# Normalising the recurrence's input behind its input product instead of ahead of it

## The chip, the cores and the metric

One core of one Trainium2 chip runs the whole program. The metric is the device time of one execution in microseconds (us), as the median of several runs.

## The reference

A trunk of two layers on 512 tokens of width 1024. Each layer adds half a SwiGLU feed-forward block, a token mixer, and half a feed-forward block again; layer 0 mixes with a gated recurrence, layer 1 with a spatial gating unit. The change lies where layer 0 passes from its first feed-forward block to the recurrence:

```python
def rms_norm(x, g):
    xf = x.astype(jnp.float32)
    y = xf * lax.rsqrt(jnp.mean(xf * xf, axis=-1, keepdims=True) + NORM_EPS)
    return (y * g.astype(jnp.float32)).astype(x.dtype)
...
def recurrent_mixer(x, w_in, conv_w, conv_b, gate_a_w, gate_a_b, gate_x_w, gate_x_b, lam, w_out):
    y, r = jnp.split(x @ w_in, 2, axis=-1)
    y = jax.nn.gelu(y)
    r = causal_depthwise_conv(r, conv_w, conv_b)
    h = rg_lru(r, gate_a_w, gate_a_b, gate_x_w, gate_x_b, lam)
    return (y * h) @ w_out
...
    h = h + 0.5 * swiglu(rms_norm(h, ffn1_norm[i]), ffn1_w_in[i], ffn1_w_out[i])
    hn = rms_norm(h, mix_norm[i])
```

The factor rsqrt(mean of squares) is one number per token; the gain g is one number per channel.

## The kernel before

Everything is float32, and each product is three matmuls: operands are split into a rounded high part and a rest, and high x high, high x low and low x high are summed. A split is one copy on ScalarE (`hi`, `whi`, `zh`; ACT in the profile) and one subtraction on VectorE (`lo`, `wlo`, `zl`; DVE). Most large products run as seven block products on 2 x 2 blocks, P1, P2, P5, P6, P3, P7 and Q4, which form sums in banks A, B, C and Q of PSUM. PSUM has six banks for these and for `r` and `gate`, and two more (`aux`) for transposes.

The kernel is written as a list of steps (`subs`). Each step has a weight tile, which is loaded and split three steps ahead, and matmuls. `hook(n, phase, fn)` puts other work at step n, in one of the phases pre, mid, rest (ahead of the step's matmuls), end and late (behind them). The order written there is the order in each engine's queue; each queue is worked off strictly in order. So work that waits on VectorE or ScalarE holds up everything behind it on that engine, the weight splits among it.

The feed-forward block's output product updates x in quarters of 256 tokens by 512 channels: A11 (tokens 0 to 255, channels 0 to 511), A12, A22, A21, in the order in which they are finished. Tokens lie on partitions in x, so the recurrence needs x transposed. In the kernel before, `TileNorm` does this a half at a time: when both quarters of a half are done, squares, a root and Newton steps give the factor `rt` of 256 tokens, four passes (two on ScalarE, two on VectorE) write normalised rows `xn`, 16 transposes put them into four banks `xt` (two of them `aux`), and eight pairs `zh`, `zl` read the banks out, with the gain, into the operand of the recurrence. `KORDER` is the order of the eight channel blocks k in that read-out and in the products.

The recurrence then has 8 blocks of 128 channels for `r` (blocks 0 to 3 first on the first half of the tokens, then on the second; 4 to 7 in one go) and 8 for `y`. An `r` block leaves its bank by one ScalarE pass (`rc`, the convolution's last tap) and three VectorE passes on the same bank (the other taps); `v` is then split, two gate products follow one or two steps later, and their sigmoids. A `y` block is copied out of its bank by VectorE (`drain`, blocks 0 to 2) and goes through gelu on ScalarE, or gelu reads the bank itself (blocks 3 to 7). `yh` multiplies it with the scanned state `h`, giving the left operand `a` of the output product, split as the first step of that product needs it.

## Time and profile before

| what | value |
|---|---|
| median of 3 runs | 1651.8 us (1651.05 to 1652.23) |
| span of the profiled execution | 1651.2 us |
| mean granted TensorE clock | 0.997 |
| TensorE matmul busy | 1621.7 us, 98% |
| VectorE busy | 1369.8 us, 83% |
| ScalarE busy | 1035.8 us, 63% |
| first `xn`, last `zl` | 345.3 us, 370.0 us |
| first `rc`, last `y` out of a bank | 375.7 us, 460.7 us |

The span is counted from the first to the last instruction of one execution; the runs' times also hold what lies around it, here 0.6 us. In rows of the time line the first number is the start in us, the second the duration (of the first to the last where several are put together, as "x8"); the bracket tells how long the engine had been idle and what ended that. Names are out<-in, with buffer numbers left out. A line number is often that of a small helper, so that the names tell more.

### The profile page before, as it was taken

What the parts mean: (1) busy time and instruction counts of PE and PEld (TensorE: products, weight loads), DVE (VectorE), ACT (ScalarE), POOL (GpSimd) and SP (SyncE); (2) the same over time, 40 slices, a digit from 0 to 9 for tenths busy, and PEclk for the clock granted to TensorE, in tenths of its full rate; (3) what the DMA queues carried; (4) which work ended last, traced back from release to release, by engine and by line L of the source; (5) the groups of instructions that cost most, each with busy time, mean ns of one, the idle gap of its engine ahead of it and who ended that gap; (6) DMA issues with size and microseconds to landing.
All of it is one profiled execution on the core that took longest, in us unless ns stands there. A gap on an engine that the chain in (4) does not pass through costs nothing. (4 is left out here: it accounts for less than half of the span.)

```text
span 1651.2 us, 20805 instructions
## 1 busy us (share of the span) xinstructions
PE 1621.7 (98%) x7475; PEld 1333.0 (81%) x7475; DVE 1369.8 (83%) x1814; ACT 1035.8 (63%) x1490; POOL 212.3 (13%) x193
## 2 busy tenths in 40 slices
PE   8999999989999999999999999999999999999997
PEld 6788888878878888888888888888888888888885
DVE  5898897787798897878988978878966988879777
ACT  6656656666957656556676565566864765665655
POOL 1111111200010111111101111111100011121120
PEclk9999999999999999999999999999999999999999
DMA  6767876952463876876838778768863557686693
GB/s 205 159 171 176 209 163 153 219 141 77 102 153 92 189 169 162 218 177 157 202 95 181 176 162 209 184 163 204 216 169 90 151 122 186 166 208 169 157 230 79
DMA packets 161288, 273.02 MB, mean 165 GB/s; under 512 B 11312, under 2 KB 37536, under 8 KB 161184
## 3 DMA queue, kind: packets, MB, share of 16 engines
q1 hardware_dynamic: 113856, 182.74, 35.9%
q0 software_dynamic: 45536, 87.10, 31.4%
q10 hardware_dynamic: 1792, 1.84, 0.4%
q8 instruction: 59, 0.97, 0.2%
q14 instruction: 45, 0.37, 0.1%
HBM read 269.55 MB, written 2.10 MB: 165 GB/s over the span
## 5 line engine op out<-in xcount | busy, mean ns | idle before, releaser
L96 ACT ACTIVATE whi<-raw 128x1024 fp32r<-128x1024 f32 (+1 forms) x539 | 556.4, 1034 | 423.0 <-PE A L347 108.2
L87 DVE TENSOR_TENSOR wlo<-raw,whi 128x1024 fp32r<-128x1024 f32 (+1 forms) x539 | 641.0, 1192 | 203.7 <-ACT whi L96 202.8
L346 PE MATMUL A<-whi,hi 128*128 128x512 f32 x984 | 393.1, 399 | 4.3 <-DVE x L93 4.3
L347 PE MATMUL A<-whi,lo 128*128 128x512 f32 x984 | 386.2, 392 | 3.6 <-DVE lo L87 3.5
L348 PE MATMUL A<-wlo,hi 128*128 128x512 f32 x984 | 385.7, 392 | 0.2 <-DVE wlo L87 0.2
L347 PEld LDWEIGHTS A<-whi,lo 128*128 128x128 f32 x984 | 185.7, 189 | 43.8 <-DVE lo L87 7.1
L346 PEld LDWEIGHTS A<-whi,hi 128*128 128x128 f32 x984 | 185.5, 189 | 41.2 <-issue 4.7
L348 PEld LDWEIGHTS A<-wlo,hi 128*128 128x128 f32 x984 | 185.6, 189 | 40.8 <-DVE wlo L87 0.6
L347 PE MATMUL C<-whi,lo 128*128 128x512 f32 x544 | 212.4, 390 | 0.9 <-DVE lo L87 0.7
L346 PE MATMUL C<-whi,hi 128*128 128x512 f32 x544 | 212.4, 390 | 0.0
L348 PE MATMUL C<-wlo,hi 128*128 128x512 f32 x544 | 211.8, 389 | 0.0
L136 POOL DMA_DIRECT2D raw<-in_ffn_w_in_dram x80 | 96.4, 1205 | 757.3 <-DVE raw L87 551.8
L87 DVE TENSOR_TENSOR raw<-raw,raw 128x1024 f32<-128x1024 f32 (+1 forms) x116 | 139.1, 1200 | 0.5
L87 DVE TENSOR_TENSOR lo<-a,hi 128x512 fp32r<-128x512 f32 (+1 forms) x196 | 127.9, 659 | 11.5 <-ACT hi L96 11.1
L136 POOL DMA_DIRECT2D raw<-in_ffn_w_out_dram x74 | 85.5, 1162 | 382.8 <-DVE wlo L87 128.1
L96 ACT ACTIVATE hi<-a 128x512 fp32r<-128x512 f32 (+1 forms) x196 | 117.5, 601 | 8.4 <-DVE a L87 6.1
L347 PEld LDWEIGHTS C<-whi,lo 128*128 128x128 f32 x544 | 102.1, 188 | 24.2 <-DVE lo L87 3.3
L346 PEld LDWEIGHTS C<-whi,hi 128*128 128x128 f32 x544 | 102.1, 188 | 21.5 <-ACT c L96 0.4
L348 PEld LDWEIGHTS C<-wlo,hi 128*128 128x128 f32 x544 | 102.1, 188 | 21.1
L96 ACT ACTIVATE c<-A 128x512 f32<-128x512 f32 x126 | 74.1, 595 | 56.9 <-PE A L348 56.5
L346 PE MATMUL B<-whi,hi 128*128 128x512 f32 x272 | 109.1, 401 | 0.0
L348 PE MATMUL B<-wlo,hi 128*128 128x512 f32 x272 | 106.2, 391 | 0.0
(169 smaller groups left out, 2182.3 us busy)
## 6 DMA issues: line engine op xcount, KB each, us to landing
raw<-in_ffn_w_in_dram SPq DMA_DIRECT2D x160, 512.0 KB, 4.4
raw<-in_ffn_w_out_dram SPq DMA_DIRECT2D x100, 512.0 KB, 5.4
raw<-in_ffn_w_in_dram POOLq DMA_DIRECT2D x80, 512.0 KB, 7.6
raw<-in_ffn_w_out_dram POOLq DMA_DIRECT2D x62, 512.0 KB, 8.3
raw<-in_sg_w_in_dram SPq DMA_DIRECT2D x18, 512.0 KB, 5.1
raw<-in_rec_w_in_dram SPq DMA_DIRECT2D x16, 512.0 KB, 3.8
raw<-in_ffn_w_in_dram SPq DMA_DIRECT2D x30, 256.0 KB, 3.6
raw<-in_ffn_w_out_dram SPq DMA_DIRECT2D x20, 256.0 KB, 4.5
```

Source lines behind the costliest of these rows:

```text
L87: nc.vector.tensor_tensor(out=o, in0=x, in1=y, op=op)
L96: nc.scalar.activation(out=o, in_=x, func=f, **k)
L136: nc.gpsimd.dma_start(out=self.v, in_=src, accum_op=ALU.add)
L346: nc.tensor.matmul(ps, zh, wh, start=fresh and i == 0, stop=False, **k)
L347: nc.tensor.matmul(ps, zl, wh, start=False, stop=False, **k)
L348: nc.tensor.matmul(ps, zh, wl, start=False, stop=end, **k)
```

## The change

`TileNorm` becomes `WideNorm`. Raw x is transposed as soon as a quarter is updated, eight transposes into the two `aux` banks, and four pairs `zh`, `zl` per quarter read them out with the gain; no factor enters. The factors of all 512 tokens are worked out once, after the last quarter; four transposes of `rt`, spread over 128 columns, give a bank in which each column holds its token's factor on all partitions, and ScalarE copies it to `S.wide` (`rtw`). An `r` block is multiplied by it on VectorE (`rn`), and `rc` and the taps read `rn`; all eight `y` blocks are drained by a multiplication with it on VectorE, and gelu works in place. `KORDER` begins with channels 4 to 7.

```diff
-KORDER = (0, 2, 4, 6, 1, 3, 5, 7)
+KORDER = (4, 5, 6, 7, 0, 1, 2, 3)
...
-    class TileNorm:
+    class WideNorm:
...
+        def turn(self, name):
+            t0, c = QUARTER[name]
+            for j in range(2):
+                ps = self.ps[name, j] = aux("xt")
                 for q in range(2):
-                    c, k = divmod(2 * j + q, 4)
+                    k = 4 * c + 2 * j + q
                     for s in range(2):
                         o = q * H + s * P
-                        nc.tensor.transpose(ps[:, o : o + P], self.xn[s, c][:, k * P : (k + 1) * P], ident)
+                        nc.tensor.transpose(ps[:, o : o + P], X[:, t0 + s, k * P : (k + 1) * P], ident)
+
+        def take(self, name):
+            t0, c = QUARTER[name]
+            cols = slice(t0 * P, t0 * P + H)
+            for j in range(2):
+                ps = self.ps.pop((name, j))
+                for q in range(2):
+                    k = 4 * c + 2 * j + q
+                    if k not in self.z:
+                        self.z[k] = (slot(F32R, "zh"), slot(F32R, "zl"))
+                    hi, lo = (t[:, cols] for t in self.z[k])
+                    src, g = ps[:, q * H : (q + 1) * H], vcol(self.grow + k)
+                    act(hi, src, AF.Copy, scale=g)
+                    stt(lo, src, g, f32(hi), ALU.mult, ALU.subtract)
+
+        def wide(self):
+            ps = self.ps["rt"] = aux("rt")
+            for t in range(TT):
+                nc.tensor.transpose(ps[:, t * P : (t + 1) * P], S.rt[:, t : t + 1].to_broadcast([P, P]), ident)
+
+        def keep(self):
+            S.wide = slot(name="rtw")
+            act(S.wide, self.ps.pop("rt"), AF.Copy)
 
         def quarter(self, name):
             n = now[0]
+            hook(n + 1, "end", lambda: self.turn(name))
+            hook(n + 2, "mid", lambda: self.take(name))
+            squares(n + 2 if name == "A21" else n + 1, "rest", name)
...
+            if name == "A21":
                 S.z = self.z
+                rstd(n, (3, "pre"), (3, "pre"), (3, "mid"))
+                hook(n + 3, "end", self.wide)
+                hook(n + 4, "mid", self.keep)
...
-            act(v, ps, AF.Identity, scale=vcol(V_CW + 24 + c), bias=vcol(V_CB + c))
+            rn = slot(name="rn")
+
+            def scaled():
+                tt(rn, ps, S.wide, ALU.mult)
+                act(v, rn, AF.Identity, scale=vcol(V_CW + 24 + c), bias=vcol(V_CB + c))
 
             def taps():
                 for k in (0, 1, 2):
-                    stt(v[:, 3 - k :], ps[:, : T - 3 + k], vcol(V_CW + 8 * k + c), v[:, 3 - k :], ALU.mult, ALU.add)
+                    stt(v[:, 3 - k :], rn[:, : T - 3 + k], vcol(V_CW + 8 * k + c), v[:, 3 - k :], ALU.mult, ALU.add)
...
         def drain(c):
             y = slot(name="y")
-            nc.vector.tensor_copy(y, ym[c])
+            tt(y, ym[c], S.wide, ALU.mult)
             ym[c] = y
 
         def gelu(c):
-            y = slot(name="y")
-            act(y, ym[c], AF.Gelu_apprx_tanh)
-            ym[c] = y
+            act(ym[c], ym[c], AF.Gelu_apprx_tanh)
...
-        plan(4, "rest", (gelu, 0, 1, 2, 3), (scan, 5, 6))
-        plan(5, "rest", (gelu, 4), (scan, 7), (yh, 0, 1))
+        plan(4, "rest", (drain, 3), (gelu, 0, 1, 2, 3), (scan, 5, 6))
+        plan(5, "rest", (drain, 4), (gelu, 4), (scan, 7), (yh, 0, 1))
```

and likewise drains 5, 6 and 7 just ahead of their gelu, at steps 6 and 7.

Three places show what this does to the queues. The first is ScalarE's read-out of the transposed banks at the end of the feed-forward block; what a row waits for stands behind it. Before, for the first half:

```order
L96 ACTIVATE whi_3136<-raw_2785 128x1024 [waits DMAHW7_49,PE_49,Activation_49]
L96 ACTIVATE zh_3140<-xt_3112,vec 128x256 [waits PE_49]
L96 ACTIVATE zh_3144<-xt_3117,vec 128x256 [waits PE_49]
L96 ACTIVATE zh_3148<-xt_3122,vec 128x256 [waits PE_49]
L96 ACTIVATE zh_3152<-xt_3127,vec 128x256 [waits PE_49]
L96 ACTIVATE zh_3156<-xt_3112,vec 128x256 [waits DVE_49]
```

Now, for quarter A11:

```order
L96 ACTIVATE hi_2936<-gw_2645 128x512 [waits DMAHW1_49,DMAHW0_49,Pool_49]
L96 ACTIVATE zh_2940<-xt_2917,vec 128x256 [waits PE_49]
L96 ACTIVATE zh_2944<-xt_2917,vec 128x256 [waits DVE_49]
L96 ACTIVATE zh_2948<-xt_2922,vec 128x256 [waits PE_49]
L96 ACTIVATE zh_2952<-xt_2922,vec 128x256 [waits DVE_49]
L96 ACTIVATE whi_2972<-raw_2677 128x1024 [waits DMAHW3_49,PE_49,Activation_49]
```

The two reads of one bank moved from four places apart to neighbours, and the second of each waits for VectorE. On VectorE at the same place, ahead of the split `lo` of A12 that the C product needs, before:

```order
L87 TENSOR_TENSOR lo_2927<-gw_2645,hi_2926 128x512
L93 SCALAR_TENSOR_TENSOR x<-C_2903,x 128x512
L93 SCALAR_TENSOR_TENSOR x<-C_2904,x 128x512
L87 TENSOR_TENSOR wlo_2947<-raw_2677,whi_2946 128x1024
L87 TENSOR_TENSOR lo_2951<-a_500_2384,hi_2950 128x512
```

and now:

```order
L87 TENSOR_TENSOR lo_2937<-gw_2645,hi_2936 128x512
L93 SCALAR_TENSOR_TENSOR zl_2941<-xt_2917,vec,zh_2940 128x256
L93 SCALAR_TENSOR_TENSOR zl_2945<-xt_2917,vec,zh_2944 128x256
L93 SCALAR_TENSOR_TENSOR zl_2949<-xt_2922,vec,zh_2948 128x256
L93 SCALAR_TENSOR_TENSOR zl_2953<-xt_2922,vec,zh_2952 128x256
L93 SCALAR_TENSOR_TENSOR x<-C_2903,x 128x512
L93 SCALAR_TENSOR_TENSOR x<-C_2904,x 128x512
L87 TENSOR_TENSOR wlo_2973<-raw_2677,whi_2972 128x1024
L87 TENSOR_TENSOR lo_2977<-a_500_2384,hi_2976 128x512
```

The four `zl` of A11 moved in ahead of the updates and of both splits. The second place is VectorE's work on r block 0. Before:

```order
L93 SCALAR_TENSOR_TENSOR rc_3397<-r_3237,vec,rc_3397 128x509
L93 SCALAR_TENSOR_TENSOR rc_3397<-r_3237,vec,rc_3397 128x510
L93 SCALAR_TENSOR_TENSOR rc_3397<-r_3237,vec,rc_3397 128x511
L87 TENSOR_TENSOR wlo_3403<-raw_2978,whi_3402 128x1024
L87 TENSOR_TENSOR lo_3407<-rc_3397,hi_3406 128x512
```

and now:

```order
L87 TENSOR_TENSOR rn_3378<-r_3212,rtw_3326 128x512
L93 SCALAR_TENSOR_TENSOR rc_3377<-rn_3378,vec,rc_3377 128x509
L93 SCALAR_TENSOR_TENSOR rc_3377<-rn_3378,vec,rc_3377 128x510
L93 SCALAR_TENSOR_TENSOR rc_3377<-rn_3378,vec,rc_3377 128x511
L87 TENSOR_TENSOR wlo_3385<-raw_3004,whi_3384 128x1024
L87 TENSOR_TENSOR lo_3389<-rc_3377,hi_3388 128x512
```

One multiplication moved in at the head, and ScalarE's `rc`, which the next row adds to, now reads its result. The third is VectorE towards the end of the y blocks, up to the first split that the output product waits for. Before:

```order
L87 TENSOR_TENSOR wlo_4127<-raw_3741,whi_4126 128x1024
L87 TENSOR_TENSOR a_868_4132<-y_4047,h_3929 128x256
L87 TENSOR_TENSOR a_869_4134<-y_4047,h_3929 128x256
L87 TENSOR_TENSOR a_868_4132<-y_4089,h_4011 128x256
L87 TENSOR_TENSOR a_869_4134<-y_4089,h_4011 128x256
L87 TENSOR_TENSOR lo_4139<-a_854_4052,hi_4138 128x512
```

and now:

```order
L87 TENSOR_TENSOR wlo_4123<-raw_3735,whi_4122 128x1024
L87 TENSOR_TENSOR y_4126<-r_4095,rtw_3326 128x512
L87 TENSOR_TENSOR a_864_4129<-y_4041,h_3925 128x256
L87 TENSOR_TENSOR a_865_4131<-y_4041,h_3925 128x256
L87 TENSOR_TENSOR a_864_4129<-y_4084,h_4005 128x256
L87 TENSOR_TENSOR a_865_4131<-y_4084,h_4005 128x256
L87 TENSOR_TENSOR lo_4136<-a_850_4047,hi_4135 128x512
```

Drain 6 (`y_4126`) stands there now, as drains 3, 4 and 5 do in the same way further up; drain 7 comes a few rows behind the last one.

## The prediction

> **What bounds the kernel now.** I began with the page's table of busy time, then asked who TensorE waited for in the stretch that the change touches (330 to 480 us: the end of the first feed-forward block, the recurrence, the start of its output product), then the windows of that stretch, then the time lines of PE, DVE and ACT in it.

> ```profile
> span 1651.2 us, 20805 instructions
> PE 1621.7 (98%) x7475; PEld 1333.0 (81%) x7475; DVE 1369.8 (83%) x1814; ACT 1035.8 (63%) x1490; POOL 212.3 (13%) x193
> ```

> TensorE is busy 98% of the span: what the change removes or adds counts only where TensorE then waits less or more. Its waits in the stretch (total, times, longest, us):

> ```profile
> PE xt L500 <- ACT xn L96: 2.7, 3, 2.1
> PE A L347 <- DVE lo L87: 2.2, 1, 2.2
> PE r L219 <- DVE zl L93: 0.9, 1, 0.9
> PE Q L347 <- DVE lo L87: 0.7, 1, 0.7
> PE C L347 <- DVE lo L87: 0.5, 1, 0.5
> ```

> Three of the five (xt, r, Q) belong to the row-wise normalisation that goes. The other two are VectorE being late, which the windows confirm (length, then busy us of PE, PEld, DVE, ACT, POOL):

> ```profile
> 330.00:340.00 10.00, 9.48 (x42) 7.25 (x41) 10.00 (x14) 6.76 (x10) 0.00 (x0) 1.00 0.85 201
> ...
> 400.00:410.00 10.00, 10.00 (x46) 8.28 (x45) 6.14 (x8) 7.62 (x13) 0.00 (x0) 1.00 0.23 76
> ...
> 450.00:460.00 10.00, 10.00 (x46) 8.29 (x45) 9.90 (x17) 6.53 (x10) 1.20 (x1) 1.00 0.43 129
> ...
> 470.00:480.00 10.00, 9.76 (x44) 7.74 (x42) 10.00 (x13) 4.74 (x6) 1.20 (x1) 1.00 0.22 60
> ```

> VectorE has nothing to spare around 335 and from 450 on, and some room between. So the stretch has three parts: the front (to the first r bank), the r blocks, and the y blocks with the start of the output product.

> **Front.** What goes, from PE's time line (start, duration, idle before and its releaser):

> ```profile
> 348.26 0.48 PE L346 MATMUL Q<-whi,hi 128*128 128x512 f32 x1
> 349.47 0.50 PE L347 MATMUL Q<-whi,lo 128*128 128x512 f32 x1 [0.72 <-DVE lo L87]
> ...
> 355.06 0.39 PE L218 MATMUL r<-zh,whi 128*128 128x256 f32 x1
> 356.36 0.39 PE L219 MATMUL r<-zl,whi 128*128 128x256 f32 x1 [0.91 <-DVE zl L93]
> ...
> 362.20 0.28 PE L220 MATMUL r<-zh,wlo 128*128 128x256 f32 x1
> 364.61 0.33 PE L500 MATMUL xt<-ident,xn 128*128 128x128 f32 x1 [2.13 <-ACT xn L96]
> 365.22 1.86 PE L500 MATMUL xt<-ident,xn 128*128 128x128 f32 x15 [0.28 <-ACT xn L96]
> ```

> From start to start, less the usual spacing (0.23, 0.12, and 0.11 for a transpose, 1.86/15 and less its tail): 1.0 at Q, 1.2 at r, 2.3 and 0.5 at xt, and 0.5 more at the first set of transposes, which has the same 0.28 wait. Together 5.4 us lost, and all of it goes, since raw x is transposed a quarter at a time with no factor to wait for.

> What comes: each quarter now brings four zh/zl pairs, and those of A11 stand on VectorE ahead of the split that the C product waits for, where VectorE is already 0.5 late. What a pair costs:

> ```profile
> 351.07 2.48 DVE L93 SCALAR_TENSOR_TENSOR x<-A,x 128x512 f32<-128x512 f32 x4
> ...
> 355.83 3.22 DVE L93 SCALAR_TENSOR_TENSOR zl<-xt,vec,zh 128x256 fp32r<-128x256 f32 x8
> ...
> 356.34 1.65 ACT L96 ACTIVATE zh<-xt,vec 128x256 fp32r<-128x256 f32 x4 [0.24 <-DVE zl L93]
> ```

> Eight zl take 3.22, so 0.39 each when they run on, with 0.48 for one alone. Before, the two readers of one bank stood four places apart, and ScalarE's fifth zh waited only 0.24 for the first zl. Now the two pairs of a bank follow each other, and the second zh waits for the first zl: from zl to zl it is 0.48 + 0.46 + two hand-overs of 0.04 = 1.0 instead of 0.39, twice in a quarter. A quarter costs VectorE 4 x 0.39 + 2 x 0.6 = 2.8, and since TensorE waits for VectorE at that place, TensorE is 2.8 later there. The eight transposes that now lie before it (8 x 0.11 = 0.9) are inside this 2.8 and fall away later. The built order has this wait at every second zh, so I count it in full; at the 0.24 of the row above the quarter would cost 0.7 less. [...]

> Two sets of transposes now wait for an update of x. Those of A22 come after the first Q piece, which ends at about 352.1 (ten matmuls 0.23 apart after 349.47), while the four updates end at 353.55: 1.4. For A21 a half piece of r (24 x 0.12 = 2.9) covers most of the way; between 0 and 1.5 I take 0.5, nearer the covered end. The four rt transposes add 0.4. The other order of k in the sums and the later squares stand where nothing waits for them. The root and Newton steps and the copy of the row are done on the way to the first r bank, two more half pieces (5.7) off: nothing, and 1 to 2 us if that cover were gone. Front: 2.8 + 1.4 + 0.5 + 0.4 - 5.4 - 0.9 = -1.2. Bounds: -4.3 with no pair wait and no wait for x; +0.9 if only the 4.3 of listed waits goes and A21 waits its full 1.5.

> **r blocks.** rn (VectorE) is put ahead of rc (ScalarE), which was released by TensorE; the taps on VectorE still follow rc. VectorE therefore stands still between rn and the taps, with everything behind it in its queue.

> ```profile
> 375.75 0.78 ACT L96 ACTIVATE rc<-r,vec 128x512 f32<-128x512 f32 x1 [6.28 <-PE r L220]
> ...
> 376.56 2.32 DVE L93 SCALAR_TENSOR_TENSOR rc<-r,vec,rc 128x509 f32<-128x509 f32 x3 [6.04 <-ACT rc L96]
> 378.80 1.22 DVE L87 TENSOR_TENSOR wlo<-raw,whi 128x1024 fp32r<-128x1024 f32 x1
> 379.93 0.69 DVE L87 TENSOR_TENSOR lo<-rc,hi 128x512 fp32r<-128x512 f32 x1
> 380.53 2.32 DVE L93 SCALAR_TENSOR_TENSOR rc<-r,vec,rc 128x509 f32<-128x509 f32 x3
> ...
> 388.93 0.69 DVE L87 TENSOR_TENSOR lo<-rc,hi 128x512 fp32r<-128x512 f32 x1 [0.99 <-ACT hi L96]
> ...
> 392.96 0.68 DVE L87 TENSOR_TENSOR pr<-rc,g 128x512 f32<-128x512 f32 x1
> ...
> 405.33 0.69 DVE L87 TENSOR_TENSOR lo<-rc,hi 128x512 fp32r<-128x512 f32 x1 [0.94 <-ACT hi L96]
> ...
> 429.04 0.69 DVE L946 COPY y<-r 128x512 f32<-128x512 f32 x1
> ...
> 400.91 0.39 PE L219 MATMUL gate<-lo,hi 128*128 128x512 f32 x1
> ```

> A block cost VectorE 376.56 to 380.53 = 4.0. Now it starts with rn, priced as the copy out of a bank at 429.04 (0.69), and the wait for rc (0.78 + two hand-overs): 1.54 more, 5.5 in all. Walk from the moment the first r bank is ready (375.75): blocks 0 and 1 take 5.5 each, block 2 5.5 and the 1.1 that its lo waits for hi behind a table load (0.99 before), block 3 6.1 with a pr of 0.6, and block 4 6.2 to the end of its lo: 29.9. TensorE needs that lo for block 4's gate at 400.91, 25.2 after. It waits 4.8, in one piece or partly at an earlier gate. Block 5 takes 1.54 + 2.24 + 1.13 + 0.6 + 1.0 (hi, as at 405.33) + 0.7 = 7.1 against 6.8 of TensorE's (24 + 6 matmuls at 0.227): 0.3 more. Blocks 6 and 7 fit. r blocks: +5.1. Bounds: 3.1 if rc from SBUF and hand-overs came 0.4 cheaper in each of five blocks, 5.5 if each hand-over is 0.08.

> **y blocks and output product.** From 432.43 VectorE runs without a gap into the output product.

> ```profile
> 432.43 0.69 DVE L87 TENSOR_TENSOR pr<-pr,tl 128x512 f32<-128x512 f32 x1 [2.71 <-ACT tl L96]
> ...
> 462.36 1.89 DVE L87 TENSOR_TENSOR lo<-a,hi 128x512 fp32r<-128x512 f32 x3
> ...
> 463.10 0.50 PE L347 MATMUL A<-whi,lo 128*128 128x512 f32 x1 [2.19 <-DVE lo L87]
> ...
> 480.81 0.50 PE L347 MATMUL A<-whi,lo 128*128 128x512 f32 x1 [1.05 <-DVE lo L87]
> ...
> 460.72 0.60 ACT L96 ACTIVATE y<-r 128x512 f32<-128x512 f32 x1
> 461.21 1.05 ACT L96 ACTIVATE whi<-raw 128x1024 fp32r<-128x1024 f32 x1
> ```

> The three copies that were there become multiplications at the same 0.6 apart. New are drains 3 to 6, ahead of the lo at 462.36 for which TensorE already waits 2.2: 4 x 0.6 = 2.4, and 0.2 since gelu, now behind the drains, hands hi over later. Drain 7 comes behind it: 0.6 more. Its gelu (0.5) and the whi queued behind it on ScalarE (1.05) end 1.6 and two hand-overs after the drain, while VectorE has one subtraction (0.6) to do before it wants that whi: 1.1. TensorE waits for VectorE again at 480.81, so these two reach it in full. y: +4.3. Bounds: 2.4 if a wait before the output product has room for the rest, 5.5.

> **Sum.** -1.2 + 5.1 + 4.3 = +8.2. The profiled run spans 1651.2, 0.6 under the median of 1651.8, so 1660.0. A measurement tells 0.2% (3.3 us) from no change.

> **Rivals.** (1) The r blocks hide rn: VectorE is only 6.1 of 10 busy at 400 to 410, as quoted, and lo of block 4 was 2.1 early. Then that term is 0: 1654.9, just inside 0.2%. Against it: the wait for rc is idle time that nothing fills, as the queue is in order. It decides where block 4's lo comes before TensorE is through block 5. Chance 0.10.

> (2) Faster: with the front at its bound of -4.3, and rn and the drains both covered by VectorE's idle time before 432.43 (2.71 there), 1647.5. It needs VectorE ahead of TensorE at 462; the row at 463.10 shows it 2.2 behind. Chance 0.05.

> (3) A half clock. A long wait late in the run is followed by matmuls 0.43 apart:

> ```profile
> 1625.79 0.47 PE L346 MATMUL A<-whi,hi 128*128 128x512 f32 x1 [4.28 <-DVE x L93]
> ...
> 1628.19 0.63 PE L347 MATMUL A<-whi,lo 128*128 128x512 f32 x1
> 1628.62 0.63 PE L348 MATMUL A<-wlo,hi 128*128 128x512 f32 x1
> ```

> At the output product TensorE will idle 2.2 + 2.6 = 4.8, so the same may follow for as long, some 3.4 us, which loses 1.7. I cost it at nothing because VectorE is then the later one up to 480; if it falls among the gates it is paid: 1661.7. Chance 0.12. [...]

> **Numbers.** The forecast itself has 0.72, from 1656.5 to 1663. Slower by over 0.2% is it and (3): 0.84; within 0.2% is (1) and the 0.01 left: 0.11; faster is (2): 0.05. The range takes in (1) below and the three upper bounds together (0.9 + 5.5 + 5.5, 1663.7) above: 1654.5 to 1664.

> **What would show it.** The waits for xn and zl are gone; xt waits for x, 1 to 2 us in all; TensorE waits 4 to 5 us at the gates for hi or lo, where it waited for nothing; VectorE stands idle 0.8 to 0.9 eight times between rn and rc; the wait at the first A matmul of the output product is 4 to 5 us. The prediction is wrong if the gates do not wait, or if VectorE turns out to have room ahead of the output product.

## The result and the profile after

The changed kernel takes 1663.8 us (median of four) where the kernel before takes 1652.0 beside it: a ratio of 1.0068, interval 1.0054 to 1.0081. One of the four executions took 9335 us, for a reason that nothing on record tells; it is left out of the ratio, and the median of the other three is 1663.4. The profiled execution spans 1662.4 us against 1651.2, so 11.2 us are to be explained; the forecast was 8.2. The page's first lines, and TensorE's waits in the changed stretch (total, times, longest, us):

```profile
span 1662.4 us, 20818 instructions
PE 1631.0 (98%) x7479; PEld 1339.5 (81%) x7479; DVE 1375.9 (83%) x1816; ACT 1034.3 (62%) x1486; POOL 212.8 (13%) x193
```
```profile
PE A L347 <- ACT hi L96: 4.6, 1, 4.6
PE gate L218 <- ACT hi L96: 2.8, 2, 2.6
PE xt L490 <- DVE x L93: 1.7, 4, 0.9
PE C L348 <- DVE lo L87: 1.5, 1, 1.5
PE gate L219 <- DVE lo L87: 1.2, 2, 0.7
PE C L347 <- ACT hi L96: 0.5, 1, 0.5
```

The waits for xn, zl and Q's lo are gone. In their place stand those that the forecast named: xt for x (1.7, of which 0.6 at the transposes of A11, which the forecast had not counted), C for a split behind the pairs (2.0), the gates for hi and lo (4.0), and 4.6 ahead of the output product. That table says who waits, not what is lost. For that I follow the same matmul through both time lines of PE (start, duration), at four places: before the front, behind it, behind the gates of blocks 4 and 5, and behind the start of the output product. First before, then after:

```profile
300.09 0.39 PE L348 MATMUL A<-wlo,hi 128*128 128x512 f32 x1
...
372.07 0.28 PE L219 MATMUL r<-zl,whi 128*128 128x256 f32 x1
...
416.10 0.39 PE L220 MATMUL r<-zh,wlo 128*128 128x512 f32 x1
...
510.01 0.40 PE L700 MATMUL p<-whi,hi 128*128 128x512 f32 x1
```
```profile
298.70 0.39 PE L349 MATMUL A<-wlo,hi 128*128 128x512 f32 x1
...
370.29 0.28 PE L219 MATMUL r<-zl,whi 128*128 128x256 f32 x1
...
422.29 0.39 PE L220 MATMUL r<-zh,wlo 128*128 128x512 f32 x1
...
520.84 0.40 PE L695 MATMUL p<-whi,hi 128*128 128x512 f32 x1
```

The changed kernel stands at -1.4 at 300, -1.8 at 372, +6.2 at 416, +10.8 at 510 and +11.2 at the end. So the front is worth -0.4, the r blocks +8.0, the y blocks +4.6; -1.4 and +0.4 come from outside the changed code. That nothing waits for the factor can be read from VectorE's first `rn`: it starts at 374.04, released by TensorE's r bank, while ScalarE has the row of factors ready at 368.8. The large surprise is in the r blocks, and the time line of PE shows it at block 4's gate:

```profile
402.92 0.80 PE L218 MATMUL gate<-hi,hi 128*128 128x512 f32 x1 [2.58 <-ACT hi L96]
404.38 0.79 PE L219 MATMUL gate<-lo,hi 128*128 128x512 f32 x1 [0.67 <-DVE lo L87]
404.98 0.63 PE L220 MATMUL gate<-hi,lo 128*128 128x512 f32 x1
405.40 0.63 PE L218 MATMUL gate<-hi,hi 128*128 128x512 f32 x1
```

The gate's matmuls last 0.63 and come 0.43 apart, not 0.39 and 0.23. The windows (length; then PE, PEld, DVE, ACT, POOL busy; then PE's granted clock) say why, cut in steps of 3.41 us:

```profile
334.38:337.79 3.41, 1.58 (x6) 1.09 (x7) 3.41 (x5) 3.38 (x6) 0.00 (x0) 1.00 0.09 26
337.79:341.20 3.41, 3.41 (x10) 2.63 (x9) 3.41 (x5) 2.03 (x3) 0.00 (x0) 0.51 0.84 250
399.27:402.68 3.41, 1.06 (x5) 0.56 (x3) 2.94 (x4) 3.41 (x6) 0.00 (x0) 1.00 0.25 76
402.68:406.09 3.41, 2.50 (x5) 1.71 (x6) 2.53 (x5) 1.31 (x3) 0.00 (x0) 0.50 0.50 144
406.09:409.50 3.41, 3.41 (x9) 2.64 (x9) 3.34 (x5) 3.41 (x6) 0.00 (x0) 0.50 0.03 10
```

Behind a step in which TensorE was busy for 1.06 or 1.58 of 3.41 us, the next one is granted half the clock. Steps at half clock are one in the front, two at the gates, and two more at the output product (470.9 to 477.8).

### The profile page after: what moved, and what is told of

It reads as the page before. It is cut to its first block, busy times and chain, and to the rows that moved or that the text cites. A ratio compares the mean times of both kernels' runs of the same rounds, so it can differ in the third digit from the quotient of the medians.

```text
span 1662.4 us, 20818 instructions
## 1 busy us (share of the span) xinstructions
PE 1631.0 (98%) x7479; PEld 1339.5 (81%) x7479; DVE 1375.9 (83%) x1816; ACT 1034.3 (62%) x1486; POOL 212.8 (13%) x193
## 5 line engine op out<-in xcount | busy, mean ns | idle before, releaser
L96 ACT ACTIVATE whi<-raw 128x1024 fp32r<-128x1024 f32 (+1 forms) x539 | 556.2, 1033 | 421.2 <-PE A L348 109.0
L87 DVE TENSOR_TENSOR wlo<-raw,whi 128x1024 fp32r<-128x1024 f32 (+1 forms) x539 | 640.2, 1190 | 200.8 <-ACT whi L96 199.3
L347 PE MATMUL A<-whi,hi 128*128 128x512 f32 x984 | 394.2, 401 | 8.1 <-ACT hi L96 4.6
L348 PE MATMUL A<-whi,lo 128*128 128x512 f32 x984 | 386.5, 393 | 0.3 <-DVE lo L87 0.2
L347 PEld LDWEIGHTS A<-whi,hi 128*128 128x128 f32 x984 | 186.1, 189 | 45.4 <-ACT hi L96 5.0
L348 PEld LDWEIGHTS A<-whi,lo 128*128 128x128 f32 x984 | 186.3, 189 | 39.4 <-DVE lo L87 2.7
L348 PE MATMUL C<-whi,lo 128*128 128x512 f32 x544 | 213.0, 391 | 2.0 <-DVE lo L87 1.7
L347 PE MATMUL C<-whi,hi 128*128 128x512 f32 x544 | 213.4, 392 | 0.5 <-ACT hi L96 0.5
L87 DVE TENSOR_TENSOR raw<-raw,raw 128x1024 f32<-128x1024 f32 (+1 forms) x116 | 138.9, 1198 | 0.5
L87 DVE TENSOR_TENSOR lo<-a,hi 128x512 fp32r<-128x512 f32 (+1 forms) x196 | 127.6, 657 | 11.5 <-ACT hi L96 11.2
L348 PEld LDWEIGHTS C<-whi,lo 128*128 128x128 f32 x544 | 102.6, 189 | 25.3 <-DVE lo L87 4.2
L347 PEld LDWEIGHTS C<-whi,hi 128*128 128x128 f32 x544 | 102.4, 188 | 22.4 <-ACT hi L96 0.9
L96 ACT ACTIVATE hi<-a 128x512 fp32r<-128x512 f32 (+1 forms) x196 | 117.2, 601 | 5.1 <-DVE a L87 2.8
L347 PE MATMUL B<-whi,hi 128*128 128x512 f32 x272 | 109.3, 402 | 0.0
L96 ACT ACTIVATE c<-A 128x512 f32<-128x512 f32 x126 | 74.1, 595 | 55.3 <-PE A L349 54.8
```

The source lines that it names most:

```text
L87: nc.vector.tensor_tensor(out=o, in0=x, in1=y, op=op)
L96: nc.scalar.activation(out=o, in_=x, func=f, **k)
L347: nc.tensor.matmul(ps, zh, wh, start=fresh and i == 0, stop=False, **k)
L348: nc.tensor.matmul(ps, zl, wh, start=False, stop=False, **k)
```

## The experiments

My theory T: the change has three terms that add. In the front the listed waits go, but pairs on one bank wait for each other; in the r blocks rn, and VectorE's wait for rc behind it, make block 4's lo late; in the y blocks four drains stand ahead of the output product's first lo. On top of that a half clock follows a long wait, and is paid where TensorE is the later engine. Rivals: only VectorE's added work counts; the front loses too; the half clock costs nothing, or is all of the excess.

All ratios are taken against runs of the kernel before on the same chip, whose median was 1652.5 beside e1 to e4, 1652.2 beside e5 to e8 and 1653.2 beside e9. The table gives, from the profiled run of each, what the front (300 to 372), the r blocks (372 to 416) and the y blocks (416 to 510) are worth against before, by the starts of the same matmuls as above; "h" marks a half clock in that stretch. A stretch that a run left alone repeats within 0.1 us, but for the +0.5 of e2, where a half clock falls into the y blocks. Outside the three stretches the profiles lie 0.4 to 3.6 us under that of before, whatever the run changed, so the terms of a row do not add up to its median.

| kernel | median us | ratio (interval) | front | r blocks | y blocks |
|---|---|---|---|---|---|
| forecast | 1660.0 | | -1.2 | +5.1 | +4.3 |
| changed kernel | 1663.8 | 1.0068 (1.0054 to 1.0081) | -0.4 h | +8.0 h | +4.6 h |
| e1 front alone | 1650.2 | 0.9990 (0.9981 to 0.9999) | -0.3 h | -0.1 | 0.0 |
| e2 before + rn | 1660.2 | 1.0047 (1.0035 to 1.0060) | 0.0 | +7.9 h | +0.5 h |
| e3 before + drains | 1656.3 | 1.0026 (1.0015 to 1.0037) | 0.0 | 0.0 | +4.1 h |
| e4 two fills | 1661.7 | 1.0060 (1.0047 to 1.0073) | -0.4 h | +5.8 | +5.7 h |
| e5 pairs apart | 1660.2 | 1.0048 (1.0035 to 1.0060) | -4.4 | +8.1 h | +4.7 h |
| e6 whi first | 1659.6 | 1.0046 (1.0033 to 1.0059) | -0.4 h | +3.0 | +5.1 h |
| e7 before, reordered | 1649.0 | 0.9981 (0.9973 to 0.9990) | -2.7 | 0.0 | 0.0 |
| e8 three fills | 1659.4 | 1.0049 (1.0035 to 1.0063) | -1.9 | +5.8 | +4.8 |
| e9 both moves | 1655.6 | 1.0013 (1.0004 to 1.0023) | -4.4 | +3.0 | +5.1 h |

**e1, the front alone.**

```diff
-                tt(rn, ps, S.wide, ALU.mult)
-                act(v, rn, AF.Identity, scale=vcol(V_CW + 24 + c), bias=vcol(V_CB + c))
+                act(v, ps, AF.Identity, scale=vcol(V_CW + 24 + c), bias=vcol(V_CB + c))
...
-        plan(4, "rest", (drain, 3), (gelu, 0, 1, 2, 3), (scan, 5, 6))
+        plan(4, "rest", (gelu, 0, 1, 2, 3), (scan, 5, 6))
```

The taps read the bank again too, and drains 4 to 7 go in the same way.

> Only the front of the change: raw x is transposed by quarters, the factors are laid out as a row. The factor is left out of r and of y 3 to 7 (rc and the taps read the bank, gelu reads the bank), so the output lacks it there. Theory T (the change costs by its r blocks and its y blocks; the front is nearly even): TensorE passes the first r bank 0 to 1.8 us earlier than before and stays so: 1650.2 to 1652.0, ratio 0.999 to 1.000, and no waits for hi or lo at the gates. Rival F (the front loses too, since the zl/zh pairs hold back the split of C): 1653 to 1655. Rival P (no two readers of a bank wait for each other): -4.3, 1647.7.

Measured: ratio 0.9990, -0.3 in the front and nothing behind it, as T has it. Rival F is out, and so is rival P, which had -4.3 (e8, below, shows -1.9 for the same front without a half clock). The gates and the output product lose only where something is added there.

**e2, rn alone on the kernel before.**

```diff
-            act(v, ps, AF.Identity, scale=vcol(V_CW + 24 + c), bias=vcol(V_CB + c))
+            def scaled():
+                tt(rn, ps, S.wide, ALU.mult)   # a tile of ones
+                act(v, rn, AF.Identity, scale=vcol(V_CW + 24 + c), bias=vcol(V_CB + c))
...
```

> The kernel before plus one thing: r is multiplied on VectorE by a tile of ones into rn, ahead of rc and the taps, which read rn. Theory T (rn plus the idle wait for rc: 1.54 more per block on VectorE's queue): block 4's lo comes 5 us too late, TensorE waits 4.5 to 5.5 us at the gates, and falls to half clock there for another 1.5 to 2.5: 1658 to 1660, ratio 1.0036 to 1.0048. Rival W (only VectorE's work counts: 5 x 0.69 = 3.4 less the 2.1 that lo was early): 1653.3. Rival H (VectorE's idle time at 400 to 410 hides it): 1652.

Measured: ratio 1.0047, +7.9 in the r blocks, with the changed kernel's waits almost to the hundredth. PE's time line:

```profile
402.44 0.79 PE L218 MATMUL gate<-hi,hi 128*128 128x512 f32 x1 [2.60 <-ACT hi L96]
403.91 0.80 PE L219 MATMUL gate<-lo,hi 128*128 128x512 f32 x1 [0.68 <-DVE lo L87]
```

T's range of 6 to 8 holds, though the listed waits at the gates add up to 4.0, under T's 4.5 to 5.5; rivals W and H (1.3 and 0) are out. The r term is rn's own, and the un-normalised front has no part in it.

**e3, the drains alone on the kernel before.** y 3 to 7 are copied out of their banks, at the places where the changed kernel multiplies them.

> The kernel before plus one thing: y 3 to 7 are copied out of their banks on VectorE ahead of gelu, where the changed kernel multiplies them. Theory T (four copies of 0.6 ahead of the output product's first lo, for which TensorE already waits; a fifth with its gelu and whi): +3.9 to +4.7: 1655.9 to 1656.7, ratio 1.0024 to 1.0028; the wait at the first A matmul of the output product grows from 2.2 to 4.6 to 4.8. If T's half clock there is paid and not hidden by VectorE: 1657.5 to 1658.5. Rival H (the first wait has room for the rest of the work): +2.4, 1654.4, or nothing, 1652.

Measured: ratio 1.0026, +4.1 in the y blocks. PE's time line at the output product's first matmul:

```profile
464.48 0.79 PE L346 MATMUL A<-whi,hi 128*128 128x512 f32 x1 [4.03 <-ACT hi L96]
```

The wait sits at this one matmul now and is 4.0, a little under what T gave it. A half clock of 6.8 us begins within this wait (at 462.66), and yet the stretch loses 4.1, not 5 to 6: here VectorE is the later engine, and the half clock is hidden.

**e4, TensorE kept busy during its two long waits.**

```diff
+    def fill(n):
+        ps = aux("fill")
+        for _ in range(n):
+            nc.tensor.matmul(ps, warm[:, :P], warm, start=True, stop=True)
...
+                if c == 4:
+                    fill(10)
...
+        hook(y0 + 7, "end", lambda: fill(20))
```

> The changed kernel plus matmuls on a tile of zeros into a bank that nobody reads: 10 ahead of block 4's gate and 20 ahead of the output product, so that TensorE is busy during most of its two long waits. Theory T (the waits of 2.6 and 0.7 us at the gates bring a half clock of 6.8 us there, which costs 2 to 2.5; the one at the output product is hidden since VectorE is then the later one): the half clock at 402 to 410 and at 471 to 478 is gone; 2 to 2.5 under the changed kernel, 1661.3 to 1661.8 where that has 1663.8 (ratio to before 1.0056 instead of 1.0071). Rival N (the half clock costs nothing, or comes without waits): 1663.8. Rival D (the half clock is the whole of the excess over the forecast and counts at both places): 4 to 5 under, 1659.3.

Measured: 1661.7, ratio 1.0060; its interval (1.0047 to 1.0073) overlaps the changed kernel's, so the stretches have to tell. The sum hides two effects. At the gates the half clock is gone and the r blocks cost 5.8 instead of 8.0: 2.2 were paid there. The one at the output product is gone too, at no gain, as expected. TensorE then came early to a later step of the product, waited 2.4 for VectorE, and got a half clock at a place where nothing hid it:

```profile
490.69 0.50 PE L355 MATMUL A<-whi,lo 128*128 128x512 f32 x1 [2.37 <-DVE lo L87]
```
```profile
488.40:491.81 3.41, 1.12 (x5) 0.94 (x6) 3.41 (x6) 1.26 (x3) 1.41 (x2) 1.00 0.72 114
491.81:495.22 3.41, 3.41 (x11) 2.66 (x10) 3.41 (x6) 2.99 (x7) 0.00 (x0) 0.50 1.03 179
```

So the y blocks cost 5.7 there. Rival N is out at the gates, rival D at the output product. That the total met T's figure is chance: ahead of the front, where a half clock at 72 falls that the changed kernel's profile does not have, the profile loses 1.0 against it, and behind the stretch it gains 2.3, of which 1.2 by a shorter half clock at the end and 0.7 by a shorter wait for x there.

**e8, a third fill ahead of that later step.** One more line: `hook(y0 + 13, "end", lambda: fill(10))`.

> The kernel with matmuls on zeros ahead of block 4's gate and of the output product, plus 10 more ahead of the seventh step of the output product, where the run with two fills waited 2.4 us and fell to half clock for 3.4. Theory T (in steps of 3.41 us on a fixed grid, TensorE runs the next step at half clock where it was busy for less than about half of the last): no half clock between 400 and 500; another 1 to 1.4 under the run with two fills: 1660 to 1660.7, ratio 1.0048 to 1.0053. Rival V (VectorE sets the time there and the half clock is hidden): as with two fills, 1661.7, ratio 1.006.

Measured: 1659.4, ratio 1.0049; no half clock from 330 to 500. The y blocks cost 4.8, not 5.7, a little less of a gain than T's 1 to 1.4; by this rival V is out, while the totals of the two runs, whose intervals overlap, would not tell. The front, in which this kernel has the changed kernel's instructions, shows -1.9 here and -0.4 in the four profiles in which a half clock fell into it. The step that decides lies a little differently from run to run:

```profile
334.20:337.60 3.40, 1.85 (x7) 1.32 (x8) 3.40 (x5) 3.37 (x6) 0.00 (x0) 1.00 0.20 47
337.60:341.00 3.40, 3.40 (x17) 2.79 (x16) 3.40 (x6) 2.64 (x4) 0.00 (x0) 1.00 0.85 240
```

TensorE was busy for 1.85 of the step here, for 1.58 in the changed kernel's profile. So this run shows the three terms bare: -1.9, +5.8, +4.8.

**e5, the pairs of a bank apart.**

```diff
-            for j in range(2):
-                ps = self.ps.pop((name, j))
-                for q in range(2):
+            for q in range(2):
+                for j in range(2):
+                    ps = self.ps[name, j]
```

> The changed kernel, with the zh/zl pairs of a quarter taken so that the two pairs of one bank stand two places apart (bank 0, bank 1, bank 0, bank 1). Theory T (ScalarE's zh and VectorE's zl wait for each other where two readers of one bank follow at once: 0.6 lost twice in each quarter, and TensorE waits for the split behind them): the split of C comes 1.2 us earlier and so does all behind it, A21's quarter may give as much again; 1.2 to 2.6 under the changed kernel. If TensorE's idle share at 334 to 338 falls below about half of 3.4 us, the half clock at 338 goes too, another 1 to 1.4: 1660 to 1662.5 in all, ratio 1.005 to 1.0063. Rival N (the pairs' order does not matter, the wait there is for x or for the bank): 1663.8, ratio 1.007.

Measured: 1660.2, ratio 1.0048. VectorE's time line at A11's quarter, the changed kernel first, then e5 (in brackets idle before and its releaser):

```profile
330.81 0.47 DVE L93 SCALAR_TENSOR_TENSOR zl<-xt,vec,zh 128x256 fp32r<-128x256 f32 x1
331.82 0.88 DVE L93 SCALAR_TENSOR_TENSOR zl<-xt,vec,zh 128x256 fp32r<-128x256 f32 x2 [0.54 <-ACT zh L96]
333.24 0.48 DVE L93 SCALAR_TENSOR_TENSOR zl<-xt,vec,zh 128x256 fp32r<-128x256 f32 x1 [0.54 <-ACT zh L96]
...
335.97 0.68 DVE L87 TENSOR_TENSOR lo<-a,hi 128x512 fp32r<-128x512 f32 x1
```
```profile
330.56 1.90 DVE L93 SCALAR_TENSOR_TENSOR zl<-xt,vec,zh 128x256 fp32r<-128x256 f32 x4
...
334.71 0.68 DVE L87 TENSOR_TENSOR lo<-a,hi 128x512 fp32r<-128x512 f32 x1
```

The two idle times of 0.54 are gone, four zl take 1.9 instead of 2.9, and C's lo starts 4.15 behind the first zl instead of 5.16, 1.0 earlier (the other 0.25 by which it leads lie ahead of the front). The front is worth -4.4 against -1.9 in e8, both without a half clock: the order of the pairs costs 2.5. Rival N is out. Part of the 2.5 are TensorE's two waits for x at the transposes of A22 and A21. The changed kernel has them, e5 has none behind 330, since there VectorE comes earlier to the updates of x too:

```profile
354.02 0.98 PE L490 MATMUL xt<-ident,x 128*128 128x128 f32 x7 [0.86 <-DVE x L93]
361.02 0.98 PE L490 MATMUL xt<-ident,x 128*128 128x128 f32 x7 [0.26 <-DVE x L93]
```

**e6, work for VectorE while it waits for rc.**

```diff
+                sub = subs[n + 1 + SPLIT_AHEAD]
+                sub.split(True)     # ScalarE: whi of the next weight
                 tt(rn, ps, S.wide, ALU.mult)
                 act(v, rn, AF.Identity, scale=vcol(V_CW + 24 + c), bias=vcol(V_CB + c))
+                sub.split()         # VectorE: its wlo, ahead of the taps
```

> The changed kernel, with one thing moved in each r block: ScalarE makes the next weight's whi before rc, and VectorE its wlo between rn and the taps, so that VectorE has work during most of its wait for rc. Theory T (the r blocks lose by that idle wait and rn together): 2.4 us less at block 4's gate, so TensorE's waits there are 0.9 and 0.5 in place of 2.6 and 0.7, under half of 3.4 us, so there is no half clock at 402 (about 1.9 more): 1659.3 to 1661.4, ratio 1.0044 to 1.0056. Rival W (only rn's work counts, the idle is made up anyway): 1663.8, ratio 1.007. Rival S (a gain at the gates is lost again at the output product, since VectorE sets the pace there): 1663.8 too, but with the waits at the gates shorter and those at the output product longer.

Measured: 1659.6, ratio 1.0046. The changed kernel's rows of one block, and e6's of another (VectorE and ScalarE):

```profile
374.04 0.69 DVE L87 TENSOR_TENSOR rn<-r,rtw 128x512 f32<-128x512 f32 x1 [6.65 <-PE r L220]
375.61 2.32 DVE L93 SCALAR_TENSOR_TENSOR rc<-rn,vec,rc 128x509 f32<-128x509 f32 x3 [0.88 <-ACT rc L96]
...
379.58 0.68 DVE L87 TENSOR_TENSOR rn<-r,rtw 128x512 f32<-128x512 f32 x1
```
```profile
397.42 0.68 DVE L87 TENSOR_TENSOR rn<-r,rtw 128x512 f32<-128x512 f32 x1
398.02 1.21 DVE L87 TENSOR_TENSOR wlo<-raw,whi 128x1024 fp32r<-128x1024 f32 x1
398.14 0.82 ACT L96 ACTIVATE rc<-rn,vec 128x512 f32<-128x512 f32 x1 [0.41 <-DVE rn L87]
399.15 2.32 DVE L93 SCALAR_TENSOR_TENSOR rc<-rn,vec,rc 128x509 f32<-128x509 f32 x3
```

The idle 0.88 is filled by wlo. TensorE's waits at the gates are then:

```profile
PE gate L231 <- ACT hi L96: 1.2, 2, 0.9
PE gate L232 <- DVE lo L87: 0.5, 2, 0.2
```

The longest is 0.9 instead of 2.6, no half clock follows, and the r blocks cost 3.0 instead of 8.0: 2.8 from VectorE's order (5.8 to 3.0), 2.2 from the clock. Rivals W and S are out: of the 5.0 gained at the gates, only 0.5 is lost again at the output product (y blocks +5.1 for +4.6).

**e7, the kernel before with another order in its front.**

```diff
-            squares(n + 1, "mid" if name == "A11" else "pre", name)
+            squares(n + 1, "mid" if name == "A11" else "rest" if name == "A22" else "pre", name)
...
-                hook(n + 3, "mid", lambda: self.take(0))
+                hook(n + 3, "pre", lambda: self.take(0))
...
-                hook(n + 2, "end", self.turn)
-                hook(n + 3, "pre", lambda: self.take(1))
+                hook(n + 3, "end", self.turn)
+                hook(n + 4, "pre", lambda: self.take(1))
```

> The kernel before, with its own row-wise normalisation, and only the order in the front moved: the first half's zh/zl are taken a phase earlier, the squares of A22 later, the second half's transposes a step later, so that TensorE waits less for xn and zl. Theory T (5.4 us are lost there to xn, zl and lo, none of which needs the change to go): 2 to 3 under the kernel before: 1649 to 1650, ratio 0.9980 to 0.9988, with the wait of 2.1 at xt cut to 1 or less. Rival N (the waits only move to the next product): 1652, ratio 1.000.

Measured: 1649.0, ratio 0.9981 (0.9973 to 0.9990). It beats both kernels, if by 0.2% only. Its waits in the front:

```profile
PE xt L500 <- ACT xn L96: 1.3, 3, 0.7
PE Q L347 <- DVE lo L87: 0.7, 1, 0.7
PE C L347 <- DVE lo L87: 0.5, 1, 0.5
```

xt waits 1.3 instead of 2.7, r for zl no more; -2.7 in the front. Half of the 5.4 us that the removed waits had cost is to be had without moving the factor.

**e9, both moves (e5 and e6) on the changed kernel.**

> The changed kernel with both moves: the two pairs of a bank two places apart, and whi and wlo of the next weight ahead of rc and the taps in each r block. Theory T (three terms that add: front, r blocks, y blocks): the front then stands at -4.4 against the kernel before, the r blocks at +2.9, the y blocks at +4.7 as in the changed kernel, since nothing was done there: +3.2, or 1655.4, ratio 1.002, give or take 1.5 for half clocks elsewhere. Rival S (the moves overlap, one place being the bound for both): no better than the better of the two alone, 1659.6, ratio 1.0045. Rival B (with both it beats the kernel before): under 1649, ratio under 0.998.

Measured: 1655.6, ratio 1.0013; -4.4, +3.0, +5.1. Front and r blocks stand where each move alone had put them, so the moves add and rival S is out, and rival B is too: it does not beat the kernel before. That 1655.6 is next to T's 1655.4 is chance in part, as the kernel before took 1653.2 on this chip: by the ratio the kernel is 2.2 slower (0.7 to 3.8), where T had 3.2. What stays is rn itself and the drains.

## Why the prediction was off, and where it was right

**The direction and the places** were right: three stretches, a front near even, r blocks and y blocks that lose. The measured time lies within 1654.5 to 1664, but at its very edge and above the 1656.5 to 1663 that had 0.72. That it lies inside is luck in part: the range took the three upper bounds together, and the r blocks went beyond theirs (8.0 for 5.5) while the front stayed well under its own (-0.4 for +0.9). What it said would show, shows, down to the 0.9 of idle between rn and rc: VectorE's group of taps in the changed stretch has 7.1 us of idle for it, eight times 0.89.

```profile
L93 DVE SCALAR_TENSOR_TENSOR rc<-rn,vec,rc 128x509 f32<-128x509 f32 (+2 forms) x24 | 18.0, 750 | 7.6 <-ACT rc L96 7.1
```

**y blocks, +4.3:** +4.6 measured, +4.8 without a half clock, +4.1 for plain copies on the kernel before. The wait of 4.6 was put at 4 to 5. The two steps of the sum show as well: in e8, without a half clock, 3.1 are lost up to the first wait (463.10 in the kernel before, 468.28 in e8), put at 2.6, and 1.7 more up to the second (480.81 and 487.73), put at 1.7. The upper bound of 5.5 was given without a working.

**Front, -1.2:** -1.9 bare. The pair price of 2.8 for a quarter measured 2.9. What was too high was the wait for x at A22 and A21: put at 1.4 and 0.5, it is 0.86 and 0.26. Nor are the two terms separate, as the sum has them: with the pairs apart both waits go, and the front gives -4.4, the lower bound that I had set for no pair wait and no wait for x.

**r blocks, +5.1:** +5.8 bare, just above the upper bound of 5.5. A block takes 5.5 as worked out (rn at 374.04, the next at 379.58). The lo of block 4 ends 30.3 after the first r bank instead of 29.9, and the bare run e4 passes that gate 5.3 later, where the walk had 4.8; then block 5 takes 0.5 where it had 0.3. (The items of block 5 add up to 7.2, not 7.1, so that 0.4 would have been the figure.)

```profile
403.65 0.68 DVE L87 TENSOR_TENSOR lo<-rc,hi 128x512 fp32r<-128x512 f32 x1
```

**The term that failed is the half clock, costed at nothing.** The reason given, that VectorE is the later engine, was right at the output product (e3, e4 and e8 show it) and was taken as if it held everywhere. At the gates TensorE sets the pace once lo is there, and the 6.8 us cost 2.2; in the front 3.4 us cost 1.5. Rival (3) named the place and the price, 1.7, too small, since I took the length of the one half clock that I had seen (3.4 us, from 1626.64 to 1630.05 in the kernel before). Of the two waits at the gates the first, 2.6 long, was enough: the half clock begins at 402.68, ahead of the second; the second, 0.7 long, falls into its first step, and the half clock lasted for another.

Against the forecast the 3.0 us are then: front 0.8 more than forecast (-0.7 by its terms, +1.5 by the clock), r blocks 2.9 more (0.7 and 2.2), y blocks 0.3 more, and -1.0 outside. There -1.6 come where the profile of before has a half clock at 73.6 that the one after has not, and 0.6 the other way elsewhere. That half clock lies far ahead of the changed code, and e4, which has the changed kernel's instructions there, shows one at 72.

## What to carry to other kernels

When a step is put between two engines whose queues run in the written order (order alone was worth 2.5 us in e5 and 2.8 in e6), price the wait for the other engine's answer along with the step, and look for work to put into it: here that wait was 0.9 of the 1.5 us more that a block took, and filling it gave back 5.0 of the 8.0 us that the r blocks had lost, 2.8 by the order and 2.2 by the half clock that then stayed away. A wait of TensorE that a change adds can cost more than its own length where TensorE is what the rest waits for: the half clock behind it cost 1.5 us for 3.4 in the front and 2.2 for 6.8 at the gates. Where VectorE was late anyway, at the output product, it cost nothing in e3 and e4. Before work is moved to another place to escape a wait, try another order at the old place.

## What the runs showed of the hardware

```profile
459.28:462.69 3.41, 1.63 (x8) 1.01 (x6) 3.41 (x7) 2.90 (x5) 0.00 (x0) 1.00 0.83 198
462.69:466.10 3.41, 3.00 (x13) 2.46 (x14) 3.41 (x7) 0.41 (x2) 1.20 (x1) 1.00 0.84 145
```

How long TensorE was busy in the step, in all, goes far to tell what followed in these runs, but does not decide alone. Cut on the grid, the profiles of the two kernels have a half clock behind each step at full clock with 0.00 to 1.61 us of busy time (1.50 at 70 in the kernel before; 1.58, above, is 1.61 where the cut is at 334.41), and behind none with 1.63 (above), 1.70 (the kernel before at 1619.8) or more. The experiments do not part there: e1 has 1.71 in the step at 335.3, and half clock behind it; e5 has 1.47 at 1627.5, and none. The step of e5, and the one behind it:

```profile
1627.54:1630.95 3.41, 1.47 (x7) 0.89 (x5) 3.41 (x6) 3.41 (x7) 0.00 (x0) 1.00 0.26 47
1630.95:1634.37 3.42, 1.08 (x5) 0.95 (x6) 3.42 (x6) 0.47 (x1) 0.00 (x0) 1.00 0.00 0
```

What else decides, these runs do not show (the ends of matmuls are modelled in the busy time), and I did not sweep it. Where a wait falls into the first step at half clock, another followed in the changed kernel's profile: with 2.50 (above), 2.51 (at 1634.9) and 2.90 (at 470.9) of 3.41 busy at half clock it stayed, and with 3.41 it ended in both kernels. Where the grid lies differs from run to run: the first starts of the two kernels, 73.57 and 337.82, are 77.4 steps apart. The same front had a half clock in four profiles and none in the fifth (e8, above, with 1.85 busy).
